# Modulation sums moved earlier in a two-block layer, and every weight remainder put on VectorE

## The chip, the cores and the metric

One Trainium2 chip, one core. The metric is the device time of one execution in microseconds (us). The kernel before took 2149.95 us, the median of 3 runs (2145.78 to 2154.07).

## The reference, cut to what matters

The input is one sequence of 256 tokens of 2048 features in float32. Two blocks run one after the other. The first has a recurrent mixer and a gated convolution FFN, and both are modulated by a vector c:

```python
mod = silu(c) @ ada_w + ada_b                       # 2048 x 12288
sh_m, sc_m, g_m, sh_f, sc_f, g_f = split(mod + ada_table, 6)
h = rms(x, norm_mix_pre) * (1 + sc_m) + sh_m        # segments 0, 1
y = rwkv7_mix(h, ...)                               # r, k, v, low-rank paths, scan, w_o
x = x + g_m * rms(y, norm_mix_post)                 # segment 2
h = rms(x, norm_ffn_pre) * (1 + sc_f) + sh_f        # segments 3, 4
u = causal_conv(h @ ffn_w_in) ; f = (silu(u[:5504]) * u[5504:]) @ ffn_w_out
x = x + g_f * rms(f, norm_ffn_post)                 # segment 5
```

The second block normalises x, projects it to 6656 columns (attention and a short convolution), projects back, and adds a gated embedding (`w_ple_gate`). All products are computed to nearly float32 precision.

## The kernel before

**How a product is computed.** Each float32 weight piece of 128 x 1024 is loaded into `raw` (L139) and split by `split` (L133 to L147) into a high part `whi` (ScalarE copy to fp32r, L142) and a remainder `wlo = raw - whi` (L146). Activations are split in the same way. Three matmuls per tile are then accumulated: high by high, low by high, high by remainder (`fm_unit` L157 to L159, `tm_units` L172 to L174). The pool has 3 buffers each of `whi` and `wlo`, and 4 of `raw` (5 from the output projection `w_o` on).

**Who computes the remainder.** L146 goes to GpSimd (POOL) when the counter `cnt` is a multiple of `share`, or when `n_pool` is above zero, and to VectorE (DVE) otherwise. Before the FFN `share` is 9999, so all go to DVE. From L1080 on `share` is 3 (it is set to 9999 at L530 and again at L959) and `n_pool` is set to `NPL` = 3 at the start of the FFN, before the second block's token-major projection (L1166) and before the gate product (L1335): the first 3 pieces there, and every third piece everywhere, are GpSimd's.

**The modulation sums.** One group (`ada_group`) is 512 columns of one segment: 8 loads of 512 KB into `raw` of pool `adap` (3 buffers), and for each 128-row slice one DVE instruction `acc += raw * sil` (L239 for the first, L245), 16 in all. A group is cut into 4 steps, and the code calls `next(ada, None)` where a step is to stand. The group ends (`fin`, `ada_fm` L280, L282) with 8 small matmuls that sum `acc` over partitions; it runs 2 steps into the next group (`ADALAG`). Segments 2 and 5 (`ada_row`) then write the 512 values to DRAM one by one (L313, to `gmd` or `gfd`), and these rows are read back as `grow`. `acc` has 2 buffers, so a group's sums can begin only when the group two ahead of it has ended. Twelve groups (segments 2, 4, 3, 48 steps) are spread over the r projection (12 steps, `RSKIP` leaves out j of 0 and 4 in each 8), the scan (26, `ASTEP`) and the output projection `w_o` (6, `OSTEP`). The last 4 run in `to_fm`, at k2 = 8 and 12, where `LATE` asks for the shift columns. Segment 5 (4 groups, 16 steps) is spread over the FFN, one step at every third j; the last step and the last `fin` stand behind the loop.

**Between `w_o` and the FFN.** `tm_out` scales the product and squares it, `add_residual` makes x (L977), `to_fm` normalises (L996), transposes on TensorE (L1000), applies scale and shift on ScalarE (`tf`, L1013), rounds `tf` to the high part on DVE (L1014) and subtracts on DVE (L1015).

**The FFN and behind it.** 43 values of j, two units each of 2 weight pieces (`fm_unit`, 48 matmuls), a convolution of 3 taps (ScalarE L1094, DVE L1095, L1096), a gate (L1108, L1109) and a split (L1110, L1111). Then `grow` is read from `gfd`, x1 is read back into `xl`, and `w_f2` runs token-major. The second block enters by `add_half` (L977) and `fm_half`, and its convolution has one GpSimd multiply `cv *= rr1` (L1307) for each of 8 j.

**What sets the order.** The kernel is written in a tile framework. Each engine runs its instructions in a fixed order; a planner makes that order from the program order as a priority, and from when, by its own cost estimates, inputs and buffers are ready. An instruction that stands late in the program is therefore placed early where its engine would be idle and its buffer is free. All loads are issued on one queue (SP).

Of the kernel before, what the change touches and what calls it, by code (L numbers as in the profile page):

```python
# [10 lines left out]
AF = mybir.ActivationFunctionType  # L11
ALU = mybir.AluOpType
# [12 lines left out]
WLEAD = 5  # L25
EARLY = (("NT", 2), ("NT", 2), ("XT", 2), ("XT", 2))
TAIL = 3
NPL = 3

SH = (9999, 9999)  # L30
A01 = (0, 1) * 6
ASTEP = (A01, A01, (0, 1, 1, 0, 1, 1, 0, 1, 1, 0, 1, 1), (1, 1, 1, 1, 1, 1, 0, 0))
OSTEP = (2, 2, 2, 0)
RSKIP = (0, 4)
PARTS = ((0, 25), (25, 32))
ADALAG = 2

# [28 lines left out]
def body(tc, A, out):  # L66
    nc = tc.nc
    top = ExitStack()
    V, S, G, PE, SP = nc.vector, nc.scalar, nc.gpsimd, nc.tensor, nc.sync
# [19 lines left out]
    def ps(tag):  # L89
        if tag == "m" and wide_m[0]:  # L90
            n_m[0] += 1
            tag = "mma"[n_m[0] % 3]
        return psp.tile([P, 512], F32, tag=tag, name="ps_" + tag, bufs=PSB[tag])

    def t_(pl, shape, tag, dt=F32, bufs=None):
        kw = {} if bufs is None else {"bufs": bufs}
        return pl.tile(shape, dt, tag=tag, name=tag, **kw)
# [34 lines left out]
    cnt, share, n_pool, n_raw = [0], [3], [0], [NRAW]  # L132
# [16 lines left out]
    def fm_unit(ap, x, acc):  # L149

        xh, xl = x
        for hf in range(2):
            wh, wl = split(ap[:, hf * 1024:(hf + 1) * 1024])
            for k in range(8):
                kt = hf * 8 + k
                sl = slice(k * P, (k + 1) * P)
                mm(acc, wh[:, sl], xh[:, kt, :], start=(kt == 0), stop=False)  # L157
                mm(acc, wh[:, sl], xl[:, kt, :], start=False, stop=False)  # L158
                mm(acc, wl[:, sl], xh[:, kt, :], start=False, stop=(kt == KT - 1))  # L159
# [36 lines left out]
    def tm_accs():  # L196
        cur = {}

        def get(nb):
            if nb not in cur:  # L200
                tg = "g" if nb % 2 == 0 else "s"
                cur[nb] = [ps(tg), ps(tg)]
            return cur[nb]
        return get
# [149 lines left out]
    for kt in range(0, KT, 2):  # L354
        ks = slice(kt, kt + 2)
# [198 lines left out]
    for j in range(NPAIR):  # L554
# [70 lines left out]
        SP.dma_start(gd[j], gs)  # L625
        if j % 8 not in RSKIP:
            next(ada, None)
# [338 lines left out]
    def rms_cols(pl, ssq, tag):  # L966
        rs = t_(pl, [P, 2], tag)
        for hf in range(2):
            V.tensor_reduce(rs[:, hf:hf + 1], ssq[:, hf, :], axis=AX.X, op=ALU.add)
            rsqrt_cols(rs[:, hf:hf + 1], rs[:, hf:hf + 1], 1.0 / D, 0)  # L970
        return rs
# [17 lines left out]
    def to_fm(pl, xt, xn, ssq, dst, scale, bias=None):  # L989

        rs = rms_cols(pl, ssq, "rsx")
        for k2 in range(0, KT, 2):
            if k2 % 4 == 0:
                ns = slice(k2 * P, (k2 + 4) * P)
                for hf in range(2):
                    V.tensor_scalar(xn[:, hf, ns], xt[:, hf, ns], rs[:, hf:hf + 1], None, op0=ALU.mult)  # L996
            p_ = ps("m")
            for i in range(2):
                for hf in range(2):
                    PE.transpose(p_[:, i * T + hf * P:i * T + (hf + 1) * P], xn[:, hf, (k2 + i) * P:(k2 + i + 1) * P], ident)  # L1000
            ks = slice(k2, k2 + 2)
            while k2 in LATE and LATE[k2] not in shifted and next(ada, 1) is None:
                pass
            if bias is None:
                for i in range(2):
                    kt, pi = k2 + i, p_[:, i * T:(i + 1) * T]
                    S.activation(dst[0][:, kt, :], pi, AF.Copy, scale=scale(kt))
                    V.scalar_tensor_tensor(dst[1][:, kt, :], pi, scale(kt), dst[0][:, kt, :],
                                           op0=ALU.mult, op1=ALU.subtract)
            else:  # L1010
                tf = t_(pl, [P, 2, T], "tf", bufs=2)
                for i in range(2):
                    S.activation(tf[:, i, :], p_[:, i * T:(i + 1) * T], AF.Identity, scale=scale(k2 + i), bias=bias(k2 + i))  # L1013
                V.tensor_copy(dst[0][:, ks, :], tf)  # L1014
                V.tensor_sub(dst[1][:, ks, :], tf, dst[0][:, ks, :])  # L1015

    def fm_raw(xt, k0, nk, dst, scale):
# [32 lines left out]
    for nb in range(4):  # L1050
# [15 lines left out]
        elif nb == 1:  # L1066
            V.tensor_copy(xt[:, 0, 0:1], accs(1)[0][:, 0:1])
            SP.dma_start(xt, A["x"].rearrange("(h p) d -> p h d", p=P))
        for _ in range(OSTEP[nb]):
            next(ada, None)  # L1070
        tm_out(po, accs(nb), nb, y2, grow, ssq)
    s2 = add_residual(po, y2, ssq, xt)
    for hf in range(2):
        SP.dma_start(x1d[hf], xt[:, hf, :])
    hx2 = new_hilo(hilo, "x")
    to_fm(po, xt, y2, s2, hx2, lambda kt: dcol(D_AF, kt), lambda kt: dcol(D_BF, kt))

    pho.close()

    share[0] = 3  # L1080
    n_pool[0] = NPL

    phf = ExitStack()
    pf = phf.enter_context(pool("pf", 1, reuse_waits="tile"))
# [4 lines left out]
    def conv(dst, src, taps, bias=None):  # L1089

        if bias is None:
            S.activation(dst, src, AF.Copy, scale=taps[2])
        else:
            S.activation(dst, src, AF.Identity, scale=taps[2], bias=bias)  # L1094
        V.scalar_tensor_tensor(dst[:, 1:], src[:, 0:T - 1], taps[1], dst[:, 1:], op0=ALU.mult, op1=ALU.add)  # L1095
        V.scalar_tensor_tensor(dst[:, 2:], src[:, 0:T - 2], taps[0], dst[:, 2:], op0=ALU.mult, op1=ALU.add)  # L1096

    for j in range(NFF):
        u = []
        for q in range(2):  # L1100
            n = 2 * j + q
            acc = ps(ftag[n % 5])
            fm_unit(A["w_f1"][n], hx2, acc[:, :T])
            u_ = t_(pf, [P, T], f"u{q}", bufs=2)
            cc = V_CONV + 4 * n
            conv(u_, acc[:, :T], [vec[:, cc + i:cc + i + 1] for i in range(3)], vec[:, cc + 3:cc + 4])
            u.append(u_)
        S.activation(u[0], u[0], AF.Silu)  # L1108
        V.tensor_tensor(u[0], u[0], u[1], op=ALU.mult)  # L1109
        S.activation(ff[0][:, j, :], u[0], AF.Copy)  # L1110
        V.tensor_sub(ff[1][:, j, :], u[0], ff[0][:, j, :])  # L1111
        if j % 3 == 0:
            next(ada, None)
    for _ in ada:
        pass
# [47 lines left out]
    S.activation(rr[:, 1, :], p_[:, :T], AF.Square)  # L1163
    rr1, rr2 = rr[:, 0, :], rr[:, 1, :]
    qkv = t_(hilo, [P, 2, 1536], "xh")
    n_pool[0] = NPL  # L1166
    accs = tm_accs()
    tm_units(A["w_i2t"], halves(h3), accs, [(nb, kt, kt == 0, kt == KT - 1) for nb in range(3) for kt in range(KT)])
    for nb in range(3):
# [99 lines left out]
    def fm_ps():  # L1269
        n_ps[0] += 1  # L1270
        return ps(ftag[n_ps[0] % 5])

    def silu2(acc):

        th_ = t_(p2, [P, T], "th2", bufs=2)
        z_ = t_(p2, [P, T], "z2")
        V.tensor_tensor(z_, acc, rr1, op=ALU.mult)
        S.activation(th_, z_, AF.Tanh, scale=0.5)
        V.scalar_tensor_tensor(th_, th_, 1.0, z_, op0=ALU.add, op1=ALU.mult)
        return th_  # L1280

    def put_mix(kt, y):
        S.activation(mxs[0][:, kt, :], y, AF.Copy)
        V.tensor_sub(mxs[1][:, kt, :], y, mxs[0][:, kt, :])
# [3 lines left out]
    for j in range(8):  # L1288
        ag = attention(j)
        cc_ = t_(p2, [P, T], "cc", bufs=2)  # L1290
        acc = fm_ps()
        fm_unit(A["w_i2f"][5 * j], h3, acc[:, :T])
        next(ag, None)
        V.tensor_tensor(cc_, acc[:, :T], rr2, op=ALU.mult)
        acc = fm_ps()
        fm_unit(A["w_i2f"][5 * j + 1], h3, acc[:, :T])
        next(ag, None)
        V.tensor_tensor(cc_, acc[:, :T], cc_, op=ALU.mult)
        cv = t_(p2, [P, T], "cv", bufs=2)
        o = V_CONV2 + 3 * j  # L1300
        conv(cv, cc_, [vec[:, o + i:o + i + 1] for i in range(3)])
        acc = fm_ps()
        fm_unit(A["w_i2f"][5 * j + 2], h3, acc[:, :T])
        next(ag, None)
        next(ag, None)
        V.tensor_tensor(cv, acc[:, :T], cv, op=ALU.mult)
        G.tensor_tensor(cv, cv, rr1, op=ALU.mult)  # L1307
        acc = fm_ps()
        fm_unit(A["w_i2f"][5 * j + 3], h3, acc[:, :T])
        next(ag, None)  # L1310
        sg = silu2(acc[:, :T])
        V.scalar_tensor_tensor(cv, cv, 0.5, sg, op0=ALU.mult, op1=ALU.mult)
        put_mix(8 + j, cv)
        acc = fm_ps()
        fm_unit(A["w_i2f"][5 * j + 4], h3, acc[:, :T])
        next(ag, None)
        sg = silu2(acc[:, :T])
        V.scalar_tensor_tensor(att[j], att[j], 0.5, sg, op0=ALU.mult, op1=ALU.mult)
        put_mix(j, att[j])
# [12 lines left out]
        fm_raw(xt, nb * 4, 4, h4, lambda kt: vcol(V_PG2, kt))  # L1332

    rs3 = rms_cols(p2, s3, "rsx")
    n_pool[0] = NPL  # L1335
    et = t_(hilo, [P, 2, D], "xh")
    for hf in range(2):
        SP.dma_start(et[:, hf, :], ed[hf])
# [155 lines left out]
```

## Time and profile before

| what | value |
|---|---|
| time of the profiled execution | 2133.21 us, span 2131.4 us |
| median of 3 runs | 2149.95 us |
| TensorE matmul busy | 1979.3 us, 93% |
| DVE busy | 1385.3 us, 65%, 2203 instructions |
| ScalarE busy | 972.3 us, 46% |
| GpSimd busy | 386.8 us, 18%; L146 there 148 times, 2460 ns each |
| L146 on DVE | 410 times, 1232 ns each |
| L245 on DVE | 240 times, 836 ns each |
| mean granted TensorE clock | 0.945 |

Busy time is what the engine's instructions cover. Matmuls are pipelined and their ends modelled, so a stage in which TensorE is held back shows more surely in the number of matmuls per microsecond than in the busy share. A duration of a DVE instruction counts from its issue, so it holds time in which the instruction stands still.

### The profile page before, as it was taken

Reading aid. Unit: us, or ns where it says so; the run is one execution under the profiler, and the core shown is the slowest. Engines: PE = TensorE matmul, PEld = TensorE weight load, DVE = VectorE, ACT = ScalarE, POOL = GpSimd, SP = SyncE. Lnnn points to the kernel's source line nnn. Section 1 sums busy time; section 2 is a strip of 40 time slices with the busy share of each in tenths; the row PEclk is TensorE's granted clock in tenths of the full one; section 3 lists DMA queues with packets and bytes.
Section 4 is the critical chain, followed back from the end, with each engine's and each line's share of the span. In section 5 each row is a group of like instructions: output and inputs, shape, how many; then the busy total and the mean of one; then the engine's idle time right before and its main releaser. Section 6 shows DMA issues by size and latency. Waiting matters only on the chain.

```text
span 2131.4 us, 36666 instructions
## 1 busy us (share of the span) xinstructions
PE 1979.3 (93%) x14708; PEld 1735.8 (81%) x14708; DVE 1385.3 (65%) x2203; ACT 972.3 (46%) x1514; POOL 386.8 (18%) x193
## 2 busy tenths in 40 slices
PE   6999989988878697899999999999989999999998
PEld 3688868886667486899999999788867899998887
DVE  3687899879778878966676766333353655656435
ACT  3544465533323244455545455344445444444453
POOL 1000000010000001323223232223232222222232
PEclk8999999998778798999999999999999999999999
DMA  8888668863667797866675766665645445456564
GB/s 279 309 273 299 208 223 293 259 182 108 151 159 214 233 324 256 278 224 191 194 251 190 213 202 196 217 192 188 195 153 170 134 166 164 159 163 208 184 201 148
DMA packets 189035, 445.25 MB, mean 209 GB/s; under 512 B 40120, under 2 KB 62776, under 8 KB 187328
## 3 DMA queue, kind: packets, MB, share of 16 engines
q1 hardware_dynamic: 188864, 442.91, 64.9%
q8 instruction: 115, 1.88, 0.4%
q14 instruction: 56, 0.46, 0.1%
HBM read 427.10 MB, written 15.75 MB: 208 GB/s over the span
## 4 chain that ended last, share of the span: by engine, by line
PE 63%; DVE 8%; DMA 6%; issue 1%; ACT 1%; SPq 0%; POOL 0%; DVEq 0%; ACTq 0%; POOLq 0%
PE ps_s L157 6%; PE ps_s L159 6%; PE ps_s L158 6%; PE ps_g L159 4%; PE ps_g L157 4%; PE ps_g L158 4%; PE ps_g L174 4%; PE ps_g L172 4%; DMA raw<-in_ada_w 4%; PE ps_g L173 4%; PE ps_s L172 4%; PE ps_s L174 4%; PE ps_s L173 4%; DVE acc L245 2%; DVE wlo L146 1%
## 5 line engine op out<-in xcount | busy, mean ns | idle before, releaser
L142 ACT ACTIVATE whi<-raw 128x1024 fp32r<-128x1024 f32 x558 | 590.1, 1059 | 665.6 <-PE ps_g L173 139.8
L146 DVE TENSOR_TENSOR wlo<-raw,whi 128x1024 fp32r<-128x1024 f32 x410 | 504.1, 1232 | 411.8 <-ACT whi L142 409.2
L146 POOL TENSOR_TENSOR wlo<-raw,whi 128x1024 fp32r<-128x1024 f32 x148 | 363.9, 2460 | 1085.7 <-ACT whi L142 1046.7
L159 PE MATMUL ps_g<-xh,wlo 128*128 128x256 f32 x816 | 233.8, 287 | 5.3 <-DVE wlo L146 5.3
L159 PE MATMUL ps_s<-xh,wlo 128*128 128x256 f32 x816 | 228.1, 279 | 7.3 <-DVE wlo L146 5.7
L157 PE MATMUL ps_g<-xh,whi 128*128 128x256 f32 x816 | 232.5, 285 | 0.5 <-ACT whi L142 0.5
L158 PE MATMUL ps_g<-xl,whi 128*128 128x256 f32 x816 | 231.4, 284 | 0.0
L157 PE MATMUL ps_s<-xh,whi 128*128 128x256 f32 x816 | 227.6, 279 | 0.0
L158 PE MATMUL ps_s<-xl,whi 128*128 128x256 f32 x816 | 227.4, 279 | 0.0
L245 DVE SCALAR_TENSOR_TENSOR acc<-raw,sil,acc 128x512 f32<-128x512 f32 x240 | 200.4, 836 | 35.3 <-DMA raw<-in_ada_w 33.6
L159 PEld LDWEIGHTS ps_g<-xh,wlo 128*128 128x128 f32 x816 | 158.0, 194 | 10.0 <-DVE wlo L146 7.5
L159 PEld LDWEIGHTS ps_s<-xh,wlo 128*128 128x128 f32 x816 | 155.0, 190 | 8.4 <-DVE wlo L146 6.5
L157 PEld LDWEIGHTS ps_g<-xh,whi 128*128 128x128 f32 x816 | 158.2, 194 | 2.7 <-issue 1.9
L158 PEld LDWEIGHTS ps_g<-xl,whi 128*128 128x128 f32 x816 | 158.0, 194 | 0.6 <-issue 0.3
L158 PEld LDWEIGHTS ps_s<-xl,whi 128*128 128x128 f32 x816 | 155.2, 190 | 0.0
L157 PEld LDWEIGHTS ps_s<-xh,whi 128*128 128x128 f32 x816 | 155.1, 190 | 0.0
L157 PE MATMUL ps_s<-h3h,whi 128*128 128x256 f32 x384 | 109.7, 286 | 0.0
L159 PE MATMUL ps_s<-h3h,wlo 128*128 128x256 f32 x384 | 108.4, 282 | 0.0
L158 PE MATMUL ps_s<-h3l,whi 128*128 128x256 f32 x384 | 108.2, 282 | 0.0
L582 POOL MEMSET ep<- 128x4 f32 x16 | 1.7, 107 | 437.9 <-DVE AR L605 225.1
L157 PEld LDWEIGHTS ps_s<-h3h,whi 128*128 128x128 f32 x384 | 72.4, 189 | 3.6 <-issue 3.5
L157 PE MATMUL ps_g<-h3h,whi 128*128 128x256 f32 x256 | 74.3, 290 | 0.0
(509 smaller groups left out, 4637.1 us busy)
## 6 DMA issues: line engine op xcount, KB each, us to landing
raw<-in_w_f SPq DMA_DIRECT2D x258, 512.0 KB, 4.6
raw<-in_ada_w SPq DMA_DIRECT2D x192, 512.0 KB, 5.3
raw<-in_w_i2f SPq DMA_DIRECT2D x80, 512.0 KB, 3.7
raw<-in_w_o SPq DMA_DIRECT2D x60, 512.0 KB, 5.1
raw<-in_w_v SPq DMA_DIRECT2D x32, 512.0 KB, 4.5
raw<-in_w_k SPq DMA_DIRECT2D x32, 512.0 KB, 5.1
raw<-in_w_r SPq DMA_DIRECT2D x32, 512.0 KB, 5.7
raw<-in_w_g SPq DMA_DIRECT2D x32, 512.0 KB, 4.8
```

What stands on the lines that cost most here:

```text
L142: S.activation(hi, raw, AF.Copy)
L146: e.tensor_sub(lo, raw, hi)
L157: mm(acc, wh[:, sl], xh[:, kt, :], start=(kt == 0), stop=False)
L158: mm(acc, wh[:, sl], xl[:, kt, :], start=False, stop=False)
L159: mm(acc, wl[:, sl], xh[:, kt, :], start=False, stop=(kt == KT - 1))
L172: mm(a, xh, wh[:, sl], start=st, stop=False)
L173: mm(a, xl, wh[:, sl], start=False, stop=False)
L174: mm(a, xh, wl[:, sl], start=False, stop=sp_)
L245: V.scalar_tensor_tensor(acc, raw[:, a, :], sc, acc, op0=ALU.mult, op1=ALU.add)
L582: G.memset(ep[:, :, 0:1], 1.0)
```

## The change

It sets the position of 4 modulation steps earlier (4 more in the r projection, 1 more in each of the first two column blocks of `w_o`, none left for `to_fm`), begins segment 5 at j = 8 with a step at every second j, rounds the high part in `to_fm` on ScalarE, and keeps L146 and the `cv` multiply on DVE throughout.

```diff
-NPL = 3
-OSTEP = (2, 2, 2, 0)
-RSKIP = (0, 4)
+OSTEP = (3, 3, 2, 0)
+RSKIP = ()
@@ to_fm
-                V.tensor_copy(dst[0][:, ks, :], tf)
+                S.activation(dst[0][:, ks, :], tf, AF.Copy)
                 V.tensor_sub(dst[1][:, ks, :], tf, dst[0][:, ks, :])
@@ before the FFN
-    share[0] = 3
-    n_pool[0] = NPL
@@ FFN loop
-        if j % 3 == 0:
+        if j >= 8 and j % 2 == 0:
             next(ada, None)
@@ second block, before w_i2t
-    n_pool[0] = NPL
@@ second block, convolution
-        G.tensor_tensor(cv, cv, rr1, op=ALU.mult)
+        V.tensor_tensor(cv, cv, rr1, op=ALU.mult)
@@ second block, before w_g2
-    n_pool[0] = NPL
```

`share` stays 9999 from L530 on, and `n_pool` is never above zero.

## Rows read from the trace of the kernel before

**Rows 1.** Windows by stage: us, busy of each engine (instructions), clock, DMA, GB/s.
```profile
300.00:456.00 156.00, 144.87 (x1009) 131.12 (x1009) 141.92 (x263) 91.45 (x187) 1.49 (x14) 0.93 0.80 257
...
720.00:820.00 100.00, 92.17 (x393) 74.32 (x391) 79.23 (x105) 35.05 (x46) 0.74 (x1) 0.93 0.83 291
...
850.00:925.00 75.00, 69.50 (x576) 68.39 (x575) 67.68 (x85) 36.06 (x50) 21.63 (x8) 0.98 0.82 273
925.00:1050.00 125.00, 125.00 (x1105) 125.00 (x1105) 77.30 (x98) 66.84 (x93) 37.88 (x16) 1.00 0.61 195
...
1355.00:1365.00 10.00, 6.23 (x17) 4.18 (x16) 2.45 (x2) 3.18 (x3) 2.30 (x1) 0.70 1.02 399
1375.00:1575.00 200.00, 200.00 (x876) 164.09 (x875) 64.01 (x55) 80.16 (x85) 57.88 (x24) 1.00 0.59 192
...
1700.00:1925.00 225.00, 225.00 (x1840) 216.31 (x1839) 135.67 (x224) 105.27 (x189) 60.20 (x29) 1.00 0.50 162
```

**Rows 2.** Timeline of DVE and POOL in the FFN: start, us, engine, line.
```profile
1263.95 0.42 DVE L1111 TENSOR_TENSOR ffl<-u,ffh 128x256 fp32r<-128x256 f32 x1
...
1274.05 2.41 DVE L1111 TENSOR_TENSOR ffl<-u,ffh 128x256 fp32r<-128x256 f32 x1 [0.48 <-ACT ffh L1110]
...
1273.78 2.40 POOL L146 TENSOR_TENSOR wlo<-raw,whi 128x1024 fp32r<-128x1024 f32 x1 [5.75 <-ACT whi L142]
```

**Rows 3.** Groups of DVE and POOL, 925 to 1325: busy, mean ns | idle before.
```profile
L146 DVE TENSOR_TENSOR wlo<-raw,whi 128x1024 fp32r<-128x1024 f32 x94 | 114.9, 1224 | 77.7 <-ACT whi L142 76.6
L1111 DVE TENSOR_TENSOR ffl<-u,ffh 128x256 fp32r<-128x256 f32 x35 | 34.1, 973 | 4.8 <-ACT ffh L1110 4.8
L245 DVE SCALAR_TENSOR_TENSOR acc<-raw,sil,acc 128x512 f32<-128x512 f32 x30 | 33.0, 1099 | 8.7 <-DMA raw<-in_ada_w 8.6
L1109 DVE TENSOR_TENSOR u<-u,u 128x256 f32<-128x256 f32 x35 | 23.1, 659 | 1.1
...
L146 POOL TENSOR_TENSOR wlo<-raw,whi 128x1024 fp32r<-128x1024 f32 x48 | 117.6, 2449 | 287.6 <-ACT whi L142 281.1 <-PE ps_s L158 6.5
```

**Rows 4.** Chain of waits, 815 to 850: start, us, what.
```profile
819.72 2.71 DVE acc L245
822.54 5.38 DVE xt L977 x2
827.92 0.61 DVE y L1044
...
841.57 0.79 PE ps_m L280 x8
```

**Rows 5.** Groups of DVE and ACT between w_o and FFN.
```profile
L1015 DVE TENSOR_TENSOR xl<-tf,xh 128x512 fp32r<-128x512 f32 x8 | 5.5, 685 | 0.1
L1014 DVE CAST xh<-tf 128x512 fp32r<-128x512 f32 x8 | 3.4, 423 | 1.1 <-ACT tf L1013 0.9
...
L1013 ACT ACTIVATE tf<-ps_m,dv 128x256 f32<-128x256 f32 x10 | 5.1, 561 | 3.0 <-PE ps_m L1000 1.7 <-DVE xl L1015 1.2
...
L142 ACT ACTIVATE whi<-raw 128x1024 fp32r<-128x1024 f32 x2 | 2.1, 1064 | 1.7 <-issue 1.7
```

**Rows 6.** Queue SP, timeline of 805 to 860: start, us, loads issued.
```profile
816.15 2.42 SPq L227 DMA_DIRECT2D raw<-in_ada_w  x2
```

**Rows 7.** Chain of waits in the scan and the FFN.
```profile
565.53 15.10 DMA raw<-in_ada_w
...
1062.83 11.92 DMA raw<-in_ada_w
...
1337.63 10.62 DMA gfd<-adav
```

**Rows 8.** Groups of DVE in the r projection, 300 to 456.
```profile
L245 DVE SCALAR_TENSOR_TENSOR acc<-raw,sil,acc 128x512 f32<-128x512 f32 x40 | 29.7, 743 | 0.0
```

**Rows 9.** Timeline of DVE at the two seams.
```profile
828.45 1.40 DVE L977 SCALAR_TENSOR_TENSOR xt<-y,rsy,xt 128x512 f32<-128x512 f32 x2
...
1578.87 8.12 DVE L977 SCALAR_TENSOR_TENSOR xl<-xh,adav,xl 128x512 f32<-128x512 f32 x3
```

## Prediction

> **What bounds the kernel now.** I read the windows by stage first. Where the FFN runs steadily TensorE makes 1105 matmuls in 125 us, 8.84 a microsecond, without a gap, and so do the FFN's output projection and the second block [rows 1]. There no other engine's time counts. What a change can win or lose lies in the other stages: the r projection, where DVE is busy 141.92 of 156 us and TensorE is held back by it; the scan; the seam between `w_o` and the FFN; the FFN's first 75 us, with 576 matmuls where 663 would fit; and 1355 to 1365, with 17 matmuls where 43.8 would fit [rows 1].
>
> Second, the timeline and the groups of DVE. An instruction with two inputs in SBUF that meets a GpSimd remainder stands still until that ends: `ffl` takes 0.42 us alone and 2.41 us beside a GpSimd remainder of 2.40 us that began 0.27 us ahead of it [rows 2]. Over 400 us of FFN (925 to 1325) the mean of `ffl` is 973 ns, of L1109 659 ns, of the modulation sum L245 1099 ns [rows 3]; free, they take 0.42 us [rows 2], as much for the same shape, and 743 ns [rows 8]. Third, the chain of waits and the timeline through the two seams, where such stretched instructions are what everything waits for [rows 4, 9].
>
> **The change part by part** (us; minus is a gain, with the two ends behind it).
>
> *Remainders back on DVE in the steady FFN.* In 400 us, 48 remainders leave GpSimd and cost DVE 48 x 1.224 = 58.8 us. What stood still goes: 35 x (0.973 - 0.42) + 35 x (0.659 - 0.42) + 30 x (1.099 - 0.743) = 19.4 + 8.4 + 10.7 = 38.5 us [rows 2, 3, 8]. DVE's net load rises by 20 us in 400, from 62% (77.30 of 125) to some 67% [rows 1]; TensorE hides it. 0 (-2 to +5: where a group of sums is bunched DVE is full).
>
> The row says that DVE is not the limit in the steady FFN. The Trainium skill (Perfetto Trace Analysis, Optimizing Scalar/DVE Operations) says that a saturated DVE can be a reason to give work to ScalarE or even GpSimd, and warns that between DVE and GpSimd it might not help. In the FFN's first 75 us DVE is busy 67.68 [rows 1]; by the advice the remainders that return there would cost what the next part gains.
>
> *FFN start.* 87 matmuls are missing in 850 to 925: 87 / 8.84 = 9.8 us [rows 1]. DVE is full there with two groups of segment 5 (32 sums of 0.743 = 24 us) and with what stands still behind 8 GpSimd remainders. Segment 5 now stands 8 j later in the program, and the last group of segment 3 ends before `to_fm`. I expect the sums to leave this stretch, and 8 x 1.224 = 9.8 us of remainders to enter. -7 (-10 to -3).
>
> *Seam between `w_o` and FFN.* On the chain stand a sum of 2.71 us, two residual instructions of 5.38 us, and then `y` of the second half, which waited behind them [rows 4]. Without GpSimd the sum takes 0.74 [rows 8] and the pair 1.40 [rows 9]: 2.0 + 4.0 = 6.0 us. The ends of two groups leave `to_fm`, of 8 matmuls in 0.79 us each [rows 4] (the row is one of the two): 1.6. Against this, the first FFN remainders come to DVE; one of them in the way costs 1.2. Rounding on ScalarE takes 8 x 0.42 from DVE and adds 8 ScalarE copies of 128 x 512. The trace has none of that shape with this output; half of `whi` (1.064 / 2) to two copies of 128 x 256 (2 x 0.561) bound it, and I take 0.55, nearer to the first [rows 5]. A pair then costs ScalarE 2 x 0.56 + 0.55 = 1.67 where DVE's 0.42 + 0.69 = 1.11 and ScalarE's 1.12 ran side by side: up to 8 x 0.55 = 4.4 slower, if nothing else were in line. I set half of it, 2.2, against the group ends' 1.6, and with a sum of 0.74 fewer in front the whole is -6.0 + 1.2 - 1.6 + 2.2 - 0.7 = -4.9: -5 (-9 to 0).
>
> *FFN output projection.* Before, the last group ended behind the loop, its row went to `gfd` (10.62 us), `grow` waited for that on queue SP, so the next `w_f2` load behind `grow` was issued that much later [rows 7]. That is the gap of 26.8 matmuls at 4.38 a microsecond: 6.1 us [rows 1]. Steps at j = 8, 10, ... reach the 17th call, the last group's end, at j = 40. The two j behind it have 192 matmuls, 22 us at 8.84, more than the 10.62. -6 (-6.1 to -4: the 2 MB of `xl` are still ahead of the load).
>
> *Ends of groups inside the FFN.* Each writes 512 values, and the next group's loads and 16 sums follow at once; the load then lands after 11.92 us [rows 7], and DVE's remainders wait behind the sum. Two such bunches stay. They are in the first line's ends.
>
> *Entry to the second block.* Three residual instructions take 8.12 us beside three GpSimd remainders; free they take 3 x 0.70, so 6.0 us less in the seam [rows 9]; one remainder of 1.22 will stand in between. -5 (-6 to -2).
>
> *Later.* Between attention and convolution, and before the gate product, other instructions with two SBUF inputs may meet a GpSimd remainder, at 2.0 us as `ffl` does [rows 2], partly repaid by a remainder on DVE. The 8 `cv` multiplies lie under a full TensorE [rows 1]. -2 (-4 to 0).
>
> *r projection.* Four more steps: 8 loads and 16 sums of 0.743 = 11.9 us of DVE, less overlap of some 0.07 each: 10.7, where DVE is the limit [rows 1, 8]. With them the end of group 1 moves from the last j to j = 10 and that of group 2 from the scan to j = 14. Each end writes 512 values to `gmd`, and the load behind it waits, 15.10 us in the scan [rows 7]. One more such end in mid-stage: +3. In all +14 (+3 to +26 = 11.9 + 15.1 - 1 for overlap).
>
> *Scan.* The same number of steps, one group further on. One of two waits like the 15.10 us [rows 7] leaves it. -5 (-12 to +4).
>
> *`w_o`.* The planner places by readiness, not only by program order: loads of segment 5 were issued at 816.15, in `w_o` [rows 6]. With `acc` free earlier, one more group (4 MB, 16 sums) falls into `w_o`, where TensorE is full and the queues move 291 GB/s [rows 1], 399 elsewhere. +2 (0 to +6).
>
> Sum: 0 - 7 - 5 - 6 - 5 - 2 + 14 - 5 + 2 = -14 us, against the profiled execution's 2133.21 (its span is 2131.4, 1.8 around it). That execution is 16.7 us below the median of the runs; since the terms are stalls, I carry -14 over to the median: 2149.95 - 14 = 2136. All gains at their far end with r projection and `w_o` at the near end give -46; all the other way, +32.
>
> **The rivals.**
> *The sums don't leave the seam* (the change doesn't do what it says). The 32 sums of segment 5, with `acc` free earlier, are placed in front of the residual, as the last group was. For it: the load at 816.15 [rows 6]. Against it: they have a lower priority than everything there. Then the seam gives 0 and the FFN start 3: -14 + 5 + 4 = -5, 2145.
> *DVE stays full at the FFN's start.* 8 remainders of 1.224 enter, 9.8 us, and what stood still behind GpSimd is no more than that [rows 1, 3]: the FFN start gives 0, the sum is -7, 2143. For it: DVE's 67.68 of 75. Against it: the 24 us of sums that are to leave.
> *The r projection pays in full* (the other side). DVE has 14 us free of 156 there, and every added sum and its wait lengthen the stage: +26, the scan returns nothing, `w_o` +6. The gains of 25 stay: +26 + 6 - 25 = +7, 2157. It decides from +19 in the r projection on, where 25 is used up. For it: 91% DVE [rows 1]; against it: the waits that it needs move, they are not new.
> *More than that.* The wait of the scan goes whole (-12), the seams give their near maximum (-8, -9, -6, -6, -4), the r projection costs 11: -34, 2116.
>
> **How the numbers follow.** Forecast (2122 to 2143) 0.46, sums in the seam 0.16, DVE full at the FFN's start 0.10, r projection in full 0.16, more 0.12. A measurement here can tell about 0.5%, 10.7 us, from no change: below 2139.2 is faster, above 2160.7 slower. From the forecast 0.36 lies below 2139.2, with the 0.12 and a little of the second and third cases 0.53; slower is half of the r projection's case with some of the unknown ends, 0.13; same 0.34. The range of 8 in 10 is 2109 to 2159.
>
> **What would show it.** GpSimd's L146 is gone and `ffl` is near 0.42 everywhere. `y` of the second half in the seam begins within 2 us of the last `w_o` matmul. Over 660 matmuls in the FFN's first 75 us. No gap before `w_f2`'s sixth load. The residual at the second block's entry is 2.1, not 8.12. The r projection is 10 to 17 us longer, the scan some 5 shorter. Wrong: sums of segment 5 between the last `w_o` matmul and the first of the FFN, an r projection over 19 us longer, or matmuls below 8.8 a microsecond in the steady FFN, DVE being late with remainders.

## The result and the profile after

The changed kernel took 2124.41 us, the median of 4 runs (2117.16 to 2130.71), beside 2147.86 (2137.68 to 2154.07) of the kernel before: ratio 0.9889, 95% interval 0.9854 to 0.9925, 23.5 us less. The forecast was 2136 (2109 to 2159). The two profiled executions differ by less, 2133.21 and 2125.33: before's lies near the low end of its runs. So totals below are of medians and ratios, and the profiles, one execution of each kernel, say where a difference lies.

I followed seven marks through the traces (start of an instruction in the timeline, us; lines of the kernel before):

| kernel | last `AR` of r projection (L605) | first `y` of `w_o` (L1044) | last `y` of `w_o` | first `ffl` (L1111) | first `y` of `w_f2` | last `y` of `w_f2` | span |
|---|---|---|---|---|---|---|---|
| before | 466 | 761 | 828 | 863 | 1402 | 1587 | 2131 |
| after | 495 | 784 | 845 | 880 | 1405 | 1584 | 2123 |
| difference, by stage | +29 | -6 | -6 | 0 | -14 | -6 | -5 |

The change loses 29 us in the r projection and gets 37 back in five of the six other stages: in these two profiles it wins 8 us. The windows of after by stage (us, busy of each engine with instructions, clock, DMA share, GB/s) answer to [rows 1]:

```profile
300.00:485.00 185.00, 154.33 (x1044) 139.55 (x1043) 153.09 (x284) 91.95 (x188) 1.59 (x15) 0.91 0.77 240
845.00:879.00 34.00, 24.67 (x187) 23.56 (x188) 33.58 (x58) 26.69 (x55) 0.00 (x0) 0.80 0.82 278
880.00:955.00 75.00, 71.96 (x621) 71.76 (x620) 60.64 (x89) 37.69 (x53) 0.00 (x0) 0.98 0.83 269
954.00:1067.00 113.00, 113.00 (x999) 113.00 (x998) 76.74 (x105) 60.74 (x84) 0.00 (x0) 1.00 0.60 193
...
1355.00:1365.00 10.00, 10.00 (x46) 8.19 (x45) 5.19 (x5) 4.05 (x4) 0.00 (x0) 1.00 0.87 322
1700.00:1925.00 225.00, 225.00 (x1840) 216.25 (x1839) 147.72 (x256) 105.91 (x187) 0.00 (x0) 1.00 0.50 162
```

The steady FFN is as full as before, 999 matmuls in 113 us or 8.84 a microsecond, with GpSimd silent, and 1355 to 1365 has no hole. The r projection is different: 185 us in which DVE is busy 153.09. Before it was full (141.92 of 156); now it stands still for 32 us. So something else than the added sums holds it.

The groups of DVE in the FFN (850 to 1330), which answer to [rows 3]:

```profile
L145 DVE TENSOR_TENSOR wlo<-raw,whi 128x1024 fp32r<-128x1024 f32 x166 | 203.0, 1223 | 111.8 <-ACT whi L141 108.8
L244 DVE SCALAR_TENSOR_TENSOR acc<-raw,sil,acc 128x512 f32<-128x512 f32 x51 | 38.0, 745 | 9.8 <-DMA raw<-in_ada_w 9.5
...
L1106 DVE TENSOR_TENSOR u<-u,u 128x256 f32<-128x256 f32 x41 | 17.4, 424 | 1.2
L1108 DVE TENSOR_TENSOR ffl<-u,ffh 128x256 fp32r<-128x256 f32 x41 | 17.1, 418 | 0.5 <-ACT ffh L1107 0.5
```

A sum takes 745 ns where it took 1099, the two others 424 and 418 where they took 659 and 973: nothing stands still any more.

### The profile page after: what moved, and what is told of

The parts are those of the page before. It is cut to its first block, busy times and chain, and to the rows that moved or that the text cites. A ratio compares the mean times of both kernels' runs of the same rounds, so it can differ in the third digit from the quotient of the medians.

```text
span 2123.4 us, 36663 instructions
## 1 busy us (share of the span) xinstructions
PE 1987.5 (94%) x14708; PEld 1744.3 (82%) x14708; DVE 1464.7 (69%) x2351; ACT 977.5 (46%) x1522; POOL 17.2 (1%) x37
## 4 chain that ended last, share of the span: by engine, by line
PE 80%; DVE 8%; DMA 6%; ACT 3%; issue 2%; SPq 0%; POOL 0%; DVEq 0%; ACTq 0%
PE ps_s L156 6%; PE ps_s L158 6%; PE ps_s L157 6%; PE ps_g L156 5%; PE ps_g L158 5%; PE ps_g L157 5%; PE ps_g L171 4%; PE ps_s L172 4%; PE ps_g L172 4%; PE ps_g L173 4%; PE ps_s L171 4%; PE ps_s L173 4%; DMA raw<-in_ada_w 3%; PE ps_a L262 2%; DVE acc L244 2%
## 5 line engine op out<-in xcount | busy, mean ns | idle before, releaser
L145 DVE TENSOR_TENSOR wlo<-raw,whi 128x1024 fp32r<-128x1024 f32 x558 | 681.8, 1223 | 414.4 <-ACT whi L141 407.1
L244 DVE SCALAR_TENSOR_TENSOR acc<-raw,sil,acc 128x512 f32<-128x512 f32 x240 | 177.5, 740 | 21.5 <-DMA raw<-in_ada_w 20.0
L158 PE MATMUL ps_g<-h3h,wlo 128*128 128x256 f32 x256 | 72.5, 283 | 1.6 <-DVE wlo L145 1.6
L158 PEld LDWEIGHTS ps_s<-h3h,wlo 128*128 128x128 f32 x384 | 72.3, 188 | 0.3 <-issue 0.3
```

Of the source, the lines that this page charges most:

```text
L145: e.tensor_sub(lo, raw, hi)
L244: V.scalar_tensor_tensor(acc, raw[:, a, :], sc, acc, op0=ALU.mult, op1=ALU.add)
```

## What the chain of waits says of the lost 29 us

The chain of after in the r projection, the scan and the FFN (start, us, what), which answers to [rows 7]:

```profile
385.50 11.73 DMA raw<-in_w_r
...
437.81 13.99 DMA vl<-vd
...
588.74 12.74 DMA raw<-in_ada_w
...
890.78 11.09 DMA raw<-in_ada_w
1189.98 12.93 DMA raw<-in_ada_w
```

Each of them starts some 2 to 6 us behind the write of a row of 512 values (SP issues those at 381.96, 436.25, 587.1, 885.4 and 1184). Before, such waits stood on `ada_w` loads in the scan and the FFN; now two stand on `w_r` and `vl`, which the r projection needs at once. The DMA view of after from 436 to 451, in 40 slices, shows what the queues do meanwhile:

```profile
GB/s 98 90 276 22 3 30 131 44 0 0 0 0 16 33 38 25 25 11 22 11 14 25 11 11 11 0 0 22 11 22 22 22 98 76 164 242 238 288 350 356
...
gmd<-adav SPq DMA_DIRECT2D x1, 2.0 KB, 10.4
```

2 KB take 10.4 us to land, and for some 9 us (slices 9 to 32) everything behind them gets 0 to 38 GB/s. My theory was now: the writes make the loss, the sums only 11 us of it; the gain is GpSimd's alone. The rival: DVE, full with sums, makes the loss, and moving the sums also makes the gain. The Trainium skill (Perfetto Trace Analysis, DMA Optimizations) says that small DMAs have a significant overhead for each transfer. The trace agrees, with 10.4 us for 2 KB in pieces of 4 bytes, and adds that the transfers behind pay too.

## Experiments

Medians of all kernels (95% interval of the ratio to before in the same session, where before took 2143.3, 2139.5 and 2139.7 us; the changed kernel was timed in another one, and the three sessions ran on different chips, so I compare ratios). The marks and the span are of one profiled execution each:

| kernel | us | ratio | last `AR` | last `y` of `w_o` | first `y` of `w_f2` | span |
|---|---|---|---|---|---|---|
| changed kernel | 2124.4 | 0.9889 (0.9854 to 0.9925) | 495 | 845 | 1405 | 2123 |
| gpsimd_off | 2110.3 | 0.9845 (0.9809 to 0.9881) | 468 | 824 | 1395 | 2112 |
| steps_only | 2152.2 | 1.0050 (1.0020 to 1.0079) | 493 | 846 | 1416 | 2143 |
| rows_whole | 2083.9 | 0.9725 (0.9692 to 0.9758) | 477 | 820 | 1371 | 2088 |
| rskip_back | 2109.5 | 0.9847 (0.9811 to 0.9883) | 467 | 826 | 1386 | 2105 |
| round_dve | 2128.7 | 0.9936 (0.9911 to 0.9960) | 498 | 845 | 1400 | 2119 |
| seg5_third | 2126.8 | 0.9951 (0.9923 to 0.9979) | 493 | 844 | 1404 | 2122 |
| before_rows_whole | 2101.0 | 0.9816 (0.9780 to 0.9852) | 469 | 809 | 1368 | 2095 |
| rows_whole_rskip | 2080.2 | 0.9716 (0.9690 to 0.9742) | 462 | 796 | 1357 | 2074 |
| gpsimd_steady | 2125.6 | 0.9917 (0.9885 to 0.9949) | 466 | 821 | 1398 | 2116 |
| gpsimd_off_rows | 2072.1 | 0.9685 (0.9654 to 0.9717) | 460 | 793 | 1349 | 2070 |
| rows_16_bytes | 2090.2 | 0.9764 (0.9728 to 0.9799) | 476 | 808 | 1360 | 2079 |
| eight_steps | 2084.1 | 0.9746 (0.9715 to 0.9777) | 453 | 813 | 1375 | 2093 |

**gpsimd_off.** One part of the change alone.

```diff
-    share[0] = 3
-    n_pool[0] = NPL          (and the two others)
-        G.tensor_tensor(cv, cv, rr1, op=ALU.mult)
+        V.tensor_tensor(cv, cv, rr1, op=ALU.mult)
```

> The kernel before with no weight remainder and no cv multiply on GpSimd, and nothing else of the change. Theory: the instructions that stood still beside GpSimd remainders are what the change wins in the seam from w_o to the FFN (5), at the FFN's start (part of 7), at the second block's entry (5) and behind it (2), so this part alone gives -12 to -20 us; the r projection keeps its 156 us, the gap of 6 us before w_f2's sixth load stays, the residual at the second block's entry is 2.1 us and not 8.12. Rival (DVE pays): the 148 remainders cost DVE as much as the standing still, the seams gain 6 at most and the FFN's start loses what the seam wins, 0 +-5 us.

It is 33 us below before, more than I expected. That is more than the 23.5 us of the whole change, though the two intervals overlap (0.9809 to 0.9881, 0.9854 to 0.9925). The r projection stays (468). In its one profile `w_o` up to its last `y` gives 4 us, the FFN 3, the stretch from the first to the last `y` of `w_f2` 6 and what follows 6, 19 in all. The edit moves the remainders and the 8 `cv` multiplies together; no run parts them. The FFN's first 75 us (windows, columns as above) are full:

```profile
860.00:935.00 75.00, 75.00 (x649) 74.97 (x648) 64.31 (x93) 38.98 (x54) 0.00 (x0) 1.00 0.83 285
```

649 matmuls in the 75 us from the first `ffl` on, where the changed kernel makes 621 and before, counted from the same mark (863 to 938), 583: the FFN's start is GpSimd's gain, 66 matmuls or 7.5 us at 8.84, and the changed kernel spoils part of it. That the whole FFN gives only 3 us in this profile is partly the slower matmul rate told in the last section: this execution has it for 250 us of the FFN, which costs some 10 us, and the one of before has none of it. The rival is refuted.

**steps_only.** The other part alone.

```diff
-OSTEP = (2, 2, 2, 0)
-RSKIP = (0, 4)
+OSTEP = (3, 3, 2, 0)
+RSKIP = ()
-        if j % 3 == 0:
+        if j >= 8 and j % 2 == 0:
```

> The kernel before with the moved modulation steps alone (four more in the r projection, one more in each of two w_o blocks, segment 5 from j = 8 on at every second j), GpSimd remainders and the rounding on DVE kept. Theory: the r projection grows by 28 us as it did in the changed kernel (156 to 185), the scan and w_o give back some 10 to 15, the gap before w_f2 (6 us) goes and the FFN's start gains some 5; in all 0 to +8 us. Rival (moving the sums is the gain): the steps alone give more than half of the 23 us by which the medians differ, -12 us or more.

It is 0.50% slower than before (0.20 to 0.79%), 4 to 17 us by the interval, at the upper end of what I expected or above it: the moved steps cost, and do not pay. The rival is refuted. The marks repeat the changed kernel's (+27 in the r projection, still +14 at `w_f2`). -33.0 and +8.9 (2152.2 against 2143.3) make -24.1; the whole change is -23.5.

**rskip_back.** The changed kernel with 12 steps in the r projection.

```diff
-RSKIP = ()
+RSKIP = (0, 4)
```

> The changed kernel with RSKIP = (0, 4) again, so that the r projection has 12 steps as before (two of the last group's steps then fall into the transposition in front of the FFN). Theory: the r projection returns to some 156 us, -28; the group that leaves it makes the scan and w_o longer by 8 to 15, and the seam by 3, so the whole is 5 to 15 us below the changed kernel. Rival (the sums cost the same wherever they stand ahead of the FFN): the whole is within 3 us of the changed kernel. Third way: the seam pays as it did before, +5 us.

The r projection is back at 467, the last `y` of `w_o` comes 19 us earlier, and that stays to the end of the span. By the medians it is 15 us below the changed kernel, by the ratios 9 (0.42%), with intervals that just overlap. With steps_only, which is slower than before clear of its interval, this speaks for leaving the four steps where they were.

**rows_whole.** The changed kernel with another write of the rows: a transpose makes 4 rows of 128 values.

```diff
-            SP.dma_start(dst[0, ...].rearrange("(k p) -> p k", p=P), r)
+            pt = ps("m")
+            PE.transpose(pt[:nk, :P], r, ident)
+            rt = t_(small, [4, P], "rt")
+            V.tensor_copy(rt[:nk, :], pt[:nk, :P])
+            SP.dma_start(dst[0, ...].rearrange("(k p) -> k p", p=P), rt[:nk, :])
```

> The changed kernel, with the 512 values of each end of segments 2 and 5 first turned into 4 rows of 128 by a transpose on TensorE and a DVE copy, so that the write to DRAM is 4 pieces of 512 bytes where it was 512 of 4 bytes. Theory: in the r projection each such end holds back the loads behind it (rows 52 and 66 GB/s in the two slices behind the write at 381.96; the w_r load behind it took 11.73, vl 13.99), and this, not the sums, is more than half of the 28 us by which the stage grew: it falls from 185 us to 160 to 170, and the whole by 15 to 30 us, the waits of 12 us on the modulation loads in scan and FFN going too. Rival (the sums): the 16 added sums and the full DVE hold the stage, it stays at 180 or more and the whole within 5 us of the changed kernel.

It is 40 us below the changed kernel by the medians, 35 by the ratios, more than I expected. With all 16 steps in it, the r projection now ends at 477: 18 us of the 29 were the rows' writes, 11 the sums (466 to 477), 16 of 0.74 us as predicted. Its window, and the DMA view of 428 to 443 where the second row is written at 429.36:

```profile
314.00:467.00 153.00, 141.35 (x977) 129.35 (x976) 140.67 (x271) 84.98 (x178) 1.49 (x14) 0.92 0.84 270
```

```profile
GB/s 336 309 208 202 276 344 291 167 198 377 333 311 333 251 279 270 325 268 336 249 191 235 164 284 344 366 388 361 333 238 287 382 380 317 336 281 257 227 218 243
```

DVE is full again (140.67 of 153), and the queues move 164 GB/s or more in every slice. The rival (the sums) is refuted for this stage, and the waits of 11 to 15 us on `ada_w` behind the rows are gone from the chain.

**rows_16_bytes.** The write straight from the 128 x 4 tile, one piece of 16 bytes for each partition.

```diff
-            SP.dma_start(dst[0, ...].rearrange("(k p) -> p k", p=P), r)
+            SP.dma_start(dst[0, ...].rearrange("(p k) -> p k", k=nk), r)
```

> The changed kernel with each row written straight from the 128 x 4 tile as 128 pieces of 16 bytes, in another order than the reference's (the gates of segments 2 and 5 are permuted, so the output differs). No transpose and no copy are added. Theory (the number of pieces sets the price): a quarter of the stall stays, the r projection is 165 to 175 us where 512 pieces made 185 and 4 pieces some 160, the whole is 25 to 35 us below the changed kernel, 2090 to 2100. Rival (any write of a row in small pieces holds the queue about as long): 2115 to 2125. Second rival (what whole rows won came from the transpose's new place for the instructions, not from the write): as the changed kernel, 2124.

It takes 2090.2 us, as expected of the number of pieces, and without a transpose, so what won is the write. But the price is not in proportion to the pieces: with a quarter of them the r projection is as short (476) as with four, and not the 165 to 175 us that I expected. The rows land after 1.5 to 6.6 us (512 pieces: 7.9 to 11.2), and in the same view, 428 to 443, 4 slices of 40 (1.5 us) are under 50 GB/s:

```profile
GB/s 281 79 128 245 4 22 123 63 0 5 60 112 341 355 295 350 355 378 392 300 377 388 432 431 360 306 350 303 183 87 197 309 358 382 320 341 320 300 255 275
```

**before_rows_whole.** The kernel before with the same edit as rows_whole.

> The kernel before with its rows of segments 2 and 5 written as 4 pieces of 512 bytes, and nothing else. Theory: the price of a row's write is paid wherever loads that are needed soon stand behind it: two ends in the r projection (399, 459), two in the scan (560, 595; waits of 15 and 13 us on the modulation loads), three in the FFN (a wait of 12 us, and the 6 us gap before w_f2): 20 to 40 us below the kernel before, with 8 to 18 of it in the r projection. Rival (the write only hurts where DVE is crowded, in the r projection with 16 steps): less than 12 us.

It is 38 us below before, as expected, but not where I said: the r projection ends at 469, no earlier than before (466), and the gain lies in the scan (the first `y` of `w_o` comes 19 us earlier) and in the FFN (another 15 to the first `y` of `w_f2`). So the two ends that the kernel before has in the r projection cost it nothing, though the queues fall to 41 and 50 GB/s behind its write at 400.26 too. The same write is paid in the scan with 12 steps and in the r projection with 16. I read this so that what counts is which loads stand behind it and how soon they are needed; no run varies that alone.

**rows_whole_rskip** and **eight_steps.** How many steps the r projection should carry once the writes are cheap.

```diff
 (rows_whole, and)                (rows_whole, and)
-RSKIP = ()                       -OSTEP = (3, 3, 2, 0) / RSKIP = ()
+RSKIP = (0, 4)                   +OSTEP = (5, 5, 2, 0) / RSKIP = (0, 2, 4, 6)
```

> The changed kernel with the rows written as 4 pieces of 512 bytes and the r projection at 12 steps (RSKIP = (0, 4)). Theory (two prices that add up, each sum ahead of the scan costs its 0.74 us of DVE and each row's write its own stall): the r projection takes some 146 us, 11 less than with 16 steps (157), the whole is 5 to 12 us below the one with whole rows alone (2084), about 2075. Rival (what 12 steps win in the changed kernel is the third row's write alone, and that is gone already): within 4 us of 2084, or above it, as the last group falls into the seam.

> The changed kernel with whole rows and 8 steps in the r projection (RSKIP = (0, 2, 4, 6)) and 5 in each of the first two blocks of w_o. Theory: with 12 steps and whole rows TensorE is busy 134 of 140 us in the r projection, so 4 steps fewer win 5 us there at most, and the group that moves on costs as much where it lands: within 5 us of the 2080 of 12 steps. Rival (DVE is still the bound): 10 to 15 us below 2080.

12 steps against 16: the r projection is 15 us shorter (462), the span 14, but the medians only 4 and the ratios 2 (0.9716, 0.9725): by the times the rival holds, and the profiles, one execution each, say otherwise. I leave it open. With 8 steps the r projection ends 9 us earlier still (453), and at the last `y` of `w_o` the kernel is 17 us behind the one with 12 (813, 796). Its 2084.1 us are within 5 of 2080, as expected: in this profile a sum that leaves the r projection is paid later.

**round_dve.** Which engine rounds in front of the FFN.

```diff
-                S.activation(dst[0][:, ks, :], tf, AF.Copy)
+                V.tensor_copy(dst[0][:, ks, :], tf)
```

> The changed kernel with the high part of the 8 pieces in front of the FFN rounded on DVE again, as before. Theory of the prediction: ScalarE's copy costs the transposition some 2 us, so the kernel is 0 to 4 us below the changed one, which five rounds can hardly tell from nothing. Rival: DVE, not ScalarE, is late in this seam, and the kernel is 3 to 6 us above the changed one.

By the medians it is 4 us above the changed kernel, by the ratios 10, with intervals that overlap. In both profiles the seam from the last `y` to the first `ffl` is 35 us (845 to 880). So the copy on ScalarE shows no loss here, against the theory, and whether it gains anything stays open.

**seg5_third.** Segment 5 as before.

```diff
-        if j >= 8 and j % 2 == 0:
+        if j % 3 == 0:
```

> The changed kernel with segment 5 at every third j again, from j = 0 on. Theory: the last group's end stands behind the loop again, its row is written late, and the gap of some 6 us before w_f2's sixth load comes back; in the FFN's first 75 us nothing more than 5 us is lost, since the changed kernel too has segment 5's sums there. In all +4 to +10 us against the changed kernel. Rival (it matters for the start as predicted, -7): +10 to +18 us. Second rival (the planner places the sums where it likes, and the gap is covered): within 2 us.

By the medians it is 2 us above the changed kernel, by the ratios 13; the intervals just overlap, so the times decide between none of the three. The windows of seg5_third:

```profile
879.00:954.00 75.00, 73.52 (x642) 73.12 (x641) 62.34 (x92) 38.39 (x54) 0.00 (x0) 1.00 0.86 275
...
1345.00:1360.00 15.00, 11.92 (x53) 9.45 (x51) 3.34 (x3) 2.12 (x2) 0.00 (x0) 0.97 0.82 272
```

The gap in front of `w_f2` is back (53 matmuls in these 15 us and 46 in the next, where 65.7 fit at 4.38 a microsecond: 2.9 + 4.5 us). But the FFN's start is better with segment 5 from j = 0, 642 matmuls against 621, and from the first `ffl` to the first `y` of `w_f2` both kernels take 525 us. So the later position does nothing for the FFN's start, against my -7: from the first `ffl` on, 22 sums stand in these 75 us in both kernels, and in the kernel before. That the gap of 7.4 us does not show in the 525 us has two reasons in these profiles: the better start, 21 matmuls or 2.4 us, and the slower matmul rate told in the last section, which the changed kernel's execution has for some 130 us there (5 us) and this one has not.

**gpsimd_steady.** gpsimd_off, with GpSimd's every third remainder back in the steady FFN.

```diff
+        if j in (8, 40):
+            share[0] = 3 if j == 8 else 9999
```

> The kernel of gpsimd_off (the kernel before, nothing on GpSimd in the FFN or behind it), with every third remainder back on GpSimd from j = 9 to j = 40 of the FFN alone. Theory of the prediction (in the steady FFN TensorE hides what stands still on DVE): 0 to +4 us against gpsimd_off's 2110, with some 8.8 matmuls a microsecond between j = 9 and 40. Rival (part of the 33 us that gpsimd_off won came out of the steady FFN): +10 us or more.

It is 0.72% above gpsimd_off by the ratios, 15 us by either measure: the theory fell, the rival holds. Two windows of gpsimd_off, the same of gpsimd_steady, and the latter's group of sums from 960 to 1290:

```profile
1050.00:1100.00 50.00, 47.89 (x407) 47.69 (x406) 39.94 (x59) 23.97 (x34) 0.00 (x0) 0.97 0.79 260
1200.00:1250.00 50.00, 49.74 (x422) 49.54 (x422) 38.35 (x54) 25.29 (x35) 0.00 (x0) 1.00 0.75 251
```

```profile
1050.00:1100.00 50.00, 46.04 (x384) 45.64 (x384) 40.11 (x51) 22.46 (x31) 13.57 (x6) 0.97 0.76 243
1200.00:1250.00 50.00, 46.28 (x392) 45.89 (x391) 38.58 (x49) 23.48 (x33) 12.36 (x5) 1.00 0.71 237
```

```profile
L245 DVE SCALAR_TENSOR_TENSOR acc<-raw,sil,acc 128x512 f32<-128x512 f32 x30 | 33.9, 1130 | 6.1 <-DMA raw<-in_ada_w 5.9
```

The loss lies in the two bunches: 23 + 30 = 53 matmuls fewer, 6.0 us at 8.84. There 16 sums follow one another with DVE's remainders behind them, and each that meets a GpSimd remainder is stretched (1130 ns in the mean, in gpsimd_off 745). Outside of the bunches TensorE hides it, as predicted (427 matmuls in both from 950 to 1000, 441 in both from 1150 to 1200). The profiles give 6 of the 15 us; where the rest goes, one execution each does not show.

**gpsimd_off_rows.** The two parts that won, and nothing else of the change.

```diff
 (before, with the edits of gpsimd_off and rows_whole)
```

> The kernel before with the two parts that won most: nothing on GpSimd in the FFN or behind it, and rows written as 4 pieces of 512 bytes; modulation steps and rounding as before. Theory (the two gains add, and the moved steps are worth nothing): 33 + 38 = 71 us below the kernel before, some 2070, below the kernel with the moved steps, whole rows and 12 steps in the r projection (2080) or level with it. Rival (they share a cause, DVE waiting with remainders behind it): 2085 to 2100.

It takes 2072.05 us, ratio 0.9685: 67.7 us below before where -33.0 and -38.5 make -71.5, so the two nearly add. It beats the kernel before and the changed one, the latter by 2% (0.9685 / 0.9889 = 0.979); against rows_whole_rskip (0.9716) the intervals overlap. The modulation steps and the rounding of the change are not in it.

## Why the prediction was right, and where it was not

The time was within the range, 12 us below the forecast. That it came so near is partly luck. In the two profiles, from which the terms were worked out, the marks add up to -8 where I had -14: the r projection cost 15 more than predicted, and the other stages gave 9 more. The medians differ by 23.5, and the 15 us between the two figures are differences between executions that no term of mine stands for. The marks give before to after by stage.

- **r projection, +14 predicted, +29 measured.** The sums were right (11 us, rows_whole). The term "one more such end in mid-stage: +3" was mis-sized: the writes make 18. I had the 15.10 us wait of the scan [rows 7] and put it at the far end of the range, because before has such ends in this stage and does not suffer from them; with 16 steps the `w_r` and `vl` loads behind them are waited for. The bound of 19, from which the rival of the r projection decides, was passed, and the total still fell, since the other stages gave 37 in the profile where I had set 25 against it.
- **Scan, -5 predicted, -6 measured** to the first `y` of `w_o`. As predicted, one of its two long waits left the chain: 15.10 [rows 7] and 12.93 us before, 12.74 after.
- **`w_o` and the seam, +2 and -5 predicted, -6 measured.** The collisions went. The timeline of DVE after, which answers to [rows 9]:

```profile
845.28 0.68 DVE L1043 TENSOR_TENSOR y<-ps_s,grow 128x512 f32<-128x512 f32 x1
845.89 1.40 DVE L976 SCALAR_TENSOR_TENSOR xt<-y,rsy,xt 128x512 f32<-128x512 f32 x2
...
848.01 3.38 DVE L976 SCALAR_TENSOR_TENSOR xt<-y,rsy,xt 128x512 f32<-128x512 f32 x5
...
856.52 1.52 DVE L244 SCALAR_TENSOR_TENSOR acc<-raw,sil,acc 128x512 f32<-128x512 f32 x2
```

  The last `w_o` matmul begins at 843.54, `y` 1.7 us later, and the residual takes its 0.70 each. But sums of segment 5 stand in this seam, a sign of being wrong that I had set, and DVE is full (33.58 of 34 us, 11.9 of it in 16 sums). The first rival, of 0.16, had the stage right, though the sums stand behind the residual and not in front of it. So the seam from the last `y` to the first `ffl` gained nothing. The groups from 845 to 880:

```profile
L244 DVE SCALAR_TENSOR_TENSOR acc<-raw,sil,acc 128x512 f32<-128x512 f32 x16 | 11.9, 746 | 0.1
...
L1013 ACT ACTIVATE xh<-tf 128x512 fp32r<-128x512 f32 x8 | 5.1, 634 | 0.1
```

  ScalarE's copy of 128 x 512, which I took as 0.55 us, is 0.634. Copies stand with 2.7 us on the seam's chain of waits (845 to 880), beside 4.0 us of remainders, where I had set one of 1.2, and 2.9 us of sums. With the rounding back on DVE (round_dve) the copies leave the chain and the seam is as long, so the copy alone does not hold it.
- **FFN to the first `y` of `w_f2`, -7 and -6 predicted, -14 measured.** The sum was right and the first reason was not. At the FFN's start 621 matmuls are made in 75 us, not over 660, and 38 more than before (583), 4.3 us. They come from GpSimd's silence (gpsimd_off: 649), not from the sums: the planner placed segment 5's there again, ahead of their position in the program. The gap at 1355 went as predicted. The rest of the 14 us no run parts: gpsimd_off has 3 us in this stage and steps_only 7. After has its four rows' writes inside the FFN (885, 1184, 1278 and 1324), before two (1062 and 1200) and two at its end (1337).
- **Remainders in the steady FFN, 0 predicted.** Right where no sums are bunched (8.84 a microsecond before and after), wrong at the two bunches: gpsimd_steady puts 15 us on it by the times, 6 of them in the trace.
- **Entry to the second block, -5 predicted, -6 measured; later, -2 and -5.** The residual, 8.12 us for three before [rows 9], is now 1.40 for the first two:

```profile
1584.30 1.40 DVE L976 SCALAR_TENSOR_TENSOR xl<-xh,adav,xl 128x512 f32<-128x512 f32 x2
```

GpSimd's part was expected as -12 to -20 and measured as -33; the moved steps as 0 to +8 and measured as +4 to +17. The traces hold -19 of the -33 only (span 2131 to 2112): before's is one of its shorter executions, and that of gpsimd_off is 4 us above its median and has the slower matmul rate for 250 us.

## What to carry to other kernels

Look behind each write in small pieces as well as at its own time: eight rows of 2 KB, each in 512 pieces of 4 bytes, cost 38 us in a kernel of 2140, paid by the loads issued behind them, and a transpose of 4 columns removed it. Where a planner places by readiness, a step that is moved later in the program may not move at all, and one that is moved earlier takes its writes along; read from the trace after where it went. When a change has several parts, time them apart: here one part gave all of the gain and another took a quarter of it back.

## What the runs showed of the hardware

Two things I had not expected. The first is the write above. The second: with a granted clock of 1.00, the 2.4 GHz level, and no idle time, TensorE makes FFN matmuls at one of two rates. Windows of rows_whole_rskip and of rows_whole in the same part of the FFN, each with one of its groups of matmuls (busy, mean ns):

```profile
908.00:1000.00 92.00, 92.00 (x783) 92.00 (x782) 60.80 (x82) 46.28 (x65) 0.00 (x0) 1.00 0.57 188
```

```profile
L156 PE MATMUL ps_s<-xh,whi 128*128 128x256 f32 x149 | 41.9, 281 | 0.0
```

```profile
930.00:1021.00 91.00, 91.00 (x805) 91.00 (x804) 61.61 (x84) 49.30 (x68) 0.00 (x0) 1.00 0.60 194
```

```profile
L156 PE MATMUL ps_s<-xh,whi 128*128 128x256 f32 x157 | 43.3, 276 | 0.0
```

8.51 a microsecond here, 8.85 there, 3.8% apart. No missing records make the difference: both traces hold 14716 matmuls. The slower rate comes in long stretches: some 310 us in rows_whole_rskip (830 to 1140), some 110 in rows_whole (1060 to 1170), some 130 in the changed kernel (1210 to 1340), two of some 150 and 100 in gpsimd_off (890 to 1045, 1225 to 1320); in the FFN of the kernel before and of seg5_third there is none. At 3.8%, 310 us of it cost some 12 us. What starts and ends it I did not test, nor whether another execution of the same kernel has it in the same place. Where one profile has it and the other not, the marks of the two differ by as much as some terms above.
